# Tokens split at 256 of 544 instead of 272, with the work list ordered anew

## The chip, the cores and the metric

The kernel runs on one core of a Trainium2 chip. The metric is the device time of one execution in microseconds (us), the median of several runs. TensorE (PE) multiplies matrices, VectorE (DVE), ScalarE (ACT) and GpSimd (POOL) do element-wise work, SyncE (SP) issues the transfers.

## The reference

One decoder step of two layers over 512 prompt tokens and 8 x 4 sample tokens, 544 tokens in all, model width 1024. Cut to its core:

```
for each of 2 layers:
    mod = silu(c) @ w_mod + b_mod            # six vectors: sh1 sc1 g1 sh2 sc2 g2
    h   = rmsnorm(x) * (1 + sc1) + sh1
    z   = h @ w_in                           # q, k, v | S5 inputs | convolution inputs
    mixed = [windowed attention | S5 state space | gated convolution + layer norm]
    x   = x + g1 * (mixed @ w_out)
    h2  = rmsnorm(x) * (1 + sc2) + sh2
    x   = x + g2 * ((silu(h2 @ w_gate) * (h2 @ w_up)) @ w_down)     # width 2816
y = rmsnorm(x)
```

## The kernel before, in words

Everything lies transposed: features on the 128 partitions, the 544 tokens along the columns. `x` is eight tiles of 128 x 544. The big products keep near-float32 accuracy by splitting both factors into a high and a low part (`fp32r`); `mm3` (L603) issues three matmuls for one product of a 128 x 128 weight block with a run of tokens: high x high, high x low, low x high. The tokens are processed in two parts, `HALVES` (L29), each of `TH` = 272 columns. `mtiles` (L608) makes one or two output tiles of one part: for every block of the contraction and every output tile, one `mm3`. The weights come in chunks of 128 x 1024 (`raw`), are rounded to `hi` by ACT or DVE, and `lo` is the difference, on POOL or DVE (`split`, L584).

The second part holds the 32 sample tokens besides prompt tokens; where these need other modulation vectors, instructions are split at `PB`, the number of prompt tokens in the second part (240 before).

A norm takes these steps for each part. `stat_tile` (L685) squares a tile of `x` and adds it to `acc`. `rstd_of` (L712) sums over the partitions and puts tokens on partitions: for every group of 128 tokens in `GRP` (L700) one matmul with the squares as the weights and a single column of ones. With 272 tokens there are three groups, at 0, 128 and 144, which overlap. Some twelve short DVE instructions (`inv_sqrt`) make the inverse root of three columns. Then one matmul per group spreads it back over all partitions, the third group with 16 columns only. `make_h` (L734) multiplies and modulates the eight tiles and splits them into high and low. There are five norms: at the start, before the feed-forward of each layer, before the second layer, and at the end.

Within a layer: `project` makes the 12 column tiles of z, and between them, in the order that `STEPS` (L219) gives, stand `s5`, `taps`, the two convolutions `c0` and `c1`, `attn`, and the convolution's layer norm `norm`. The output projection contracts `mix`: tiles 0 and 1 are S5, 2 to 5 attention, 6 and 7 the convolution, in this order. It and the down projection take the last three tiles of the first part and then the last three of the second part (`SEQ_END`, L1482), so that the first part's norm can run beside the second part's matmuls. The last pair of the feed-forward's start is arranged likewise: two column tiles of the first part, then two of the second.

The order of all instructions on each engine is made when the program is built. `_schedule` (L225) is a list scheduler with estimated costs (`_cost`, L154): an instruction's rank is its longest path to the end plus a lift that its stage was given (`LIFTS`, L216, in ns). When an engine is free, the ready instruction of highest rank goes next; where two engines may take it, the scheduler picks one. `MODS` (L210) says which pairs of the six modulation vectors are computed together. Where PE has nothing ready for 60 ns, the scheduler puts in filler matmuls on the tile `zeros` (L627), so a wait of PE that the scheduler foresees appears in the trace as filler, not as idle time. Almost every instruction has the line L111 in the profile, that of the recording helper, so the rows below are told apart by tile names and shapes. A float32 matmul that isn't fp32r stands in the trace as two instructions.

Of the kernel before, what the change touches and what calls it, by code (L numbers as in the profile page):

```python
# [13 lines left out]
I32 = mybir.dt.int32  # L14
# [5 lines left out]
P = 128  # L20
# [3 lines left out]
NP = 512  # L24
# [1 line left out]
NT = 4  # L26
T = NP + NB * NT
TH = T // 2
HALVES = ((0, TH), (TH, T))  # L29
PB = NP - TH  # L30
DFF = 2816
MF = DFF // P
FH = MF // 2
# [185 lines left out]
STEPS = (((0, 1, 2), "taps", (3,), "c0", (4,), (5,), (6,), (7,), (8,), (9,), "s5", "attn", (10, 11), "c1", "norm"),  # L219
# [5 lines left out]
def _schedule(order, tags):  # L225
# [110 lines left out]
    wait = [len(d) for d in dep]  # L336
    bank = [sorted({a.tensor.name for a in o[1] + o[2] if a.space == PSUM}) for o in ops]
    lock = {}
    pick, why, last_dep, slot_by, freed_by, prev_end, prev_op = [0] * N, {}, {}, {}, {}, {}, {}
    engs = sorted({e for o in ops for e, _ in o[0]})  # L340
    pool = {e: [] for e in engs}
# [15 lines left out]
    while done < N - len(spare):  # L357
        progress = True
        while progress:
            progress = False  # L360
            for e in engs:
# [1 line left out]
                    continue  # L363
                best = None
                for r, i in pool[e]:
                    if not all(len(free[tags[n][0]]) > min(bisect.bisect_left(todo[tags[n][0]], nth[n]), RESERVE.get(tags[n][0], 99))
                               for n in touch[i] if n not in held):
                        continue
                    p = [o[0] for o in ops[i][0]].index(e)
                    key = -r  # L370
                    late = max((lock[b][0] for b in bank[i] if b in lock and lock[b][1] != e), default=0.0)
                    if late > now:
                        heapq.heappush(ev, (late, -1, 2))
                        continue
                    if len(ops[i][0]) > 1:
                        here = now + cost[i][p]
                        if port[i][p]:
                            here = max(here, held_port["Pool" if e == "DVE" else "DVE"] + cost[i][p])
                        if any(max(at[o[0]], now) + sum(cost[v][0] for w, v in pool[o[0]] if w < r) + cost[i][q] < here + (MARGIN if q < p else 0.0)
                               for q, o in enumerate(ops[i][0]) if q < p):  # L380
                            continue
                    if e == "ACT":
                        f = _TABLES.get(ops[i][3][p].get("func"))
                        if f and table not in f:
                            key -= 3000.0
                    if best is None or key > best[0]:
                        best = (key, r, i, p)
                if best is None and e == "PE" and FILL and spare and NWU <= issued < reals and now >= at[e] + (0.0 if filled else FILL):
                    late = max((lock[b][0] for b in bank[spare[-1]] if b in lock and lock[b][1] != e), default=0.0)
                    if late > now:  # L390
# [104 lines left out]
def tile_decoder_step(ctx: ExitStack, tc: tile.TileContext, I, O, order, dbg=None, stop=99):  # L495
# [26 lines left out]
    def small(cols, tag, bufs=2, dt=F32):  # L522
        return new(sm, [P, cols], dt, tag, bufs)

    def wt_(n=TH):
        return small(TH, "w", bufs=NWT)[:, :n]
# [80 lines left out]

    def mtiles(blks, acts, *hs):  # L608

        pss = [[mbank()[:, :TH] for _ in blks] for _ in hs]  # L610
        n = len(acts)
        order.stream = True
        for k in range(n):
# [71 lines left out]
    def stat_tile(acc, k, h):  # L685
# [1 line left out]
        if k == 0:  # L687
            act(acc, x[k][:, c0:c1], AF.Square)
        elif isinstance(acc, list):
            acc.append(wt_())  # L690
            act(acc[-1], x[k][:, c0:c1], AF.Square)
        else:
            sq = wt_()
            act(sq, x[k][:, c0:c1], AF.Square)
            tt(acc, acc, sq, ADD, eng=VG)

    def new_acc(h):
        return small(TH, f"acc{h}", bufs=1)

    GRP = (0, P, TH - P)  # L700

    def inv_sqrt(v, r, t, si, steps):

# [8 lines left out]
    def rstd_of(acc, n=D, last=False):  # L712


        bk = mbank()
        parts = acc if isinstance(acc, list) else [acc]
        for i, a_ in enumerate(parts):
            for g, o in enumerate(GRP):
                PE.matmul(out=bk[:, 4 * i + g:4 * i + g + 1], lhsT=a_[:, o:o + P], rhs=ones[:, 0:1], start=True, stop=True)
        v, r, t = (small(3, f"rs{i}") for i in range(3))  # L720
        ts(v, bk[:, 0:3], 1.0 / n, MUL, EPS, ADD)
        for i in range(1, len(parts)):
            stt(v, bk[:, 4 * i:4 * i + 3], 1.0 / n, v, MUL, ADD)
        if last:
            V.reciprocal(out=t, in_=v)
            act(r, t, AF.Sqrt)
        inv_sqrt(v, r, t, None if last else small(3, "rsi", dt=I32), 1 if last else 3)
        out = bk[:, P:P + TH]
        for g, o in enumerate(GRP):
            c = 0 if g < 2 else 2 * P - o  # L730
            PE.matmul(out=out[:, o + c:o + P], lhsT=r[:, g:g + 1].broadcast_to((P, P)), rhs=ident[:, c:], start=True, stop=True)
        return out

    def make_h(hp, rs, gt, modT, vsh, h):  # L734
        c0, c1 = HALVES[h]
        for k in range(KD):
            t = wt_()
            tt(t, x[k][:, c0:c1], rs, MUL, eng=V if rs.space == PSUM else VG)
            hf = wt_()
            npc = TH if h == 0 else PB  # L740
# [260 lines left out]
    rs0 = [rs0[:, i * TH:(i + 1) * TH] for i in range(2)]  # L1001
    for h in range(2):
        cp(rs0[h], rstd_of(accs[h]))
    prm, taps = ssm_params(0)
# [11 lines left out]
    for l in range(L):  # L1016
# [32 lines left out]

        def rope(out, ps, h):  # L1050
            c0, c1 = HALVES[h]
            sw = wt_()
            for b in range(4):
                cp(sw[32 * b:32 * b + 32], ps[32 * (b ^ 1):32 * (b ^ 1) + 32])
            t = wt_()
# [4 lines left out]
        def glu_out(i, h, pa, pg_):  # L1060

            c0 = HALVES[h][0]
            th = wt_()
            act(th, pg_, AF.Tanh, scale=0.5)
            ts(th, th, 0.5, MUL, 0.5, ADD, eng=VG)
            n, j0 = (TH if h == 0 else PB), CB + c0 // CS
# [7 lines left out]
        def z_out(role, h, ps):  # L1074
            c0, c1 = HALVES[h]
            i = int(role[1])
            if role[0] == "u":
                n = TH // 4 if h == 0 else PB // 4
# [387 lines left out]

        def resid(m, h, ps, gv):
            c0, c1 = HALVES[h]
            n = TH if h == 0 else PB
# [30 lines left out]
        for hf in range(2):  # L1500
# [2 lines left out]

            def gate_up(m, h, pss):
                c0, c1 = HALVES[h]
                sg = wt_()
                act(sg, pss[0], AF.Silu)
                av = wt_()
                tt(av, sg, pss[1], MUL)
                hi = at[m][0][:, c0:c1]  # L1510
                cp(hi, av)
# [27 lines left out]

    for h in range(2):  # L1540
        c0, c1 = HALVES[h]
        o = [page()[:, :4 * TH].rearrange("p (k t) -> p k t", k=4) for _ in range(2)]
        order.lift = FLIFT * (1 - h)
        for k in range(KD):
            act(o[k // 4][:, k % 4], x[k][:, c0:c1], AF.Copy, scale=par[0][:, A_GF + k:A_GF + k + 1])
        rs = rstd_of(accs[h], last=True)
        rsc = wt_()
        cp(rsc, rs)
        for k in range(0, KD, 2):
            v = o[k // 4][:, k % 4:k % 4 + 2]  # L1550
            if k == 4:
                tt(v, v, bc(rsc, 1, 2), MUL, eng=G)
            else:
                tt(v, v, bc(rs, 1, 2), MUL)
        for k in (0, 2, 6, 4):
            Q.dma_start(out=O["y"][:, k:k + 2, c0:c1], in_=o[k // 4][:, k % 4:k % 4 + 2])

    order.issue(tc)

# [190 lines left out]
```

## Time and profile before

| | us |
|---|---|
| median of 3 runs | 1311.04 |
| lowest, highest | 1310.49, 1311.4 |
| the profiled execution | 1313.35 |
| its span, first to last instruction | 1311.5 |
| PE busy in it | 1295.5 |
| DVE, ACT, POOL busy | 723.6, 431.5, 368.6 |

The profiled execution's time is its span and 1.85 us around it, and lies 2.3 us above the median. A busy PE counts fillers as work and each group of overlapping matmuls from the first start to the last end.

### The profile page before, as it was taken

The page shows a single profiled execution, that of the slowest core. Times are in us where ns is not written, and L with a number is a line of the kernel's source. Part 1 is how long each engine was busy: PE and PEld are TensorE (multiplying, and loading weights), DVE is VectorE, ACT ScalarE, POOL GpSimd, SP SyncE. Part 2 cuts the span into 40 slices and gives each one's busy share as a digit, 9 for nine tenths or more (in the row PEclk, how much of TensorE's full clock was granted, in tenths as well). Part 3 has the DMA queues.
Part 4 walks back from the last instruction along what each step waited for, and adds up shares of the span by engine and source line. Part 5 has one row for each costly group of instructions (what it writes and reads, how often), then busy time and mean ns, then how long its engine had stood idle before and what let it go on. Part 6 is the DMA issues. An engine that isn't in the chain of part 4 may idle for free.

```text
span 1311.5 us, 25293 instructions
## 1 busy us (share of the span) xinstructions
PE 1295.5 (99%) x10328; PEld 1219.6 (93%) x10328; DVE 723.6 (55%) x1674; ACT 431.5 (33%) x928; POOL 368.6 (28%) x455
## 2 busy tenths in 40 slices
PE   8999999999999999999999999999999999999997
PEld 7888768999999999999988897899999999999997
DVE  6868884676743357433447868657434323344343
ACT  4533471453221122212226346345312112122232
POOL 8653220248432033322012412022223202233101
PEclk9998999999999999999999999999999999999999
DMA  9886785523222223223366672231232222232322
GB/s 333 288 278 210 235 235 197 182 101 97 97 83 96 81 81 97 95 75 105 108 213 233 229 279 69 95 99 49 97 97 96 82 81 83 95 97 81 97 65 69
DMA packets 79654, 176.56 MB, mean 135 GB/s; under 512 B 22769, under 2 KB 40497, under 8 KB 79537
## 3 DMA queue, kind: packets, MB, share of 16 engines
q1 hardware_dynamic: 79536, 174.94, 40.6%
q8 instruction: 81, 1.33, 0.4%
q14 instruction: 37, 0.30, 0.1%
HBM read 164.22 MB, written 10.70 MB: 133 GB/s over the span
## 4 chain that ended last, share of the span: by engine, by line
PE 90%; DVE 3%; DMA 2%; POOL 2%; issue 1%; SPq 1%; ACT 1%; POOLq 0%; ACTq 0%; DVEq 0%
PE ps_s L111 86%; PE mod_s L111 4%; DVE pg_s L111 2%; POOL sp_s L111 1%; SPq L111 1%; POOL pg_s L111 1%; DVE sp_s L111 1%; DMA raw_s<-w_in 1%; DMA wm_s<-w_mod 1%; DMA pg_s<-d_s 0%; DMA conv_out<-pg_s 0%; ACT pg_s L111 0%; DMA pg_s<-ssm 0%; POOL w_s L111 0%; POOLq L1743 0%
## 5 line engine op out<-in xcount | busy, mean ns | idle before, releaser
L111 PE MATMUL ps_s<-pg_s,hi_s 128*128 128x272 f32 x5504 | 1050.8, 290 | 1.4 <-DVE pg_s L111 1.1
L111 PEld LDWEIGHTS ps_s<-pg_s,hi_s 128*128 128x128 f32 x5504 | 865.1, 189 | 18.6 <-issue 13.8
L111 PE MATMUL ps_s<-pg_s,lo_s 128*128 128x272 f32 x2752 | 791.2, 289 | 0.0
L111 PEld LDWEIGHTS ps_s<-pg_s,lo_s 128*128 128x128 f32 x2752 | 518.7, 189 | 7.0 <-issue 6.9
L111 POOL TENSOR_TENSOR lo_s<-raw_s,hi_s 128x1024 fp32r<-128x1024 f32 x77 | 223.3, 2903 | 657.8 <-DVE hi_s L111 372.0
L111 ACT ACTIVATE hi_s<-raw_s 128x1024 fp32r<-128x1024 f32 x128 | 135.0, 1059 | 356.2 <-PE ps_s L111 313.6
L111 DVE TENSOR_TENSOR lo_s<-raw_s,hi_s 128x1024 fp32r<-128x1024 f32 x95 | 119.7, 1261 | 63.9 <-ACT hi_s L111 62.4
L111 DVE TENSOR_TENSOR pg_s<-w_s,pg_s 128x272 fp32r<-128x272 f32 x148 | 113.3, 775 | 37.4 <-ACT pg_s L111 37.0
L111 PE MATMUL ps_s<-pg_s,pg_s 128*128 128x104 f32 (+10 forms) x864 | 123.5, 317 | 2.9 <-DVE nmx_s L111 1.7
L111 ACT ACTIVATE w_s<-ps_s 128x272 f32<-128x272 f32 (+1 forms) x178 | 69.0, 388 | 165.0 <-PE ps_s L111 145.6
L111 PEld LDWEIGHTS ps_s<-pg_s,pg_s 128*128 128x128 f32 (+4 forms) x864 | 97.1, 182 | 27.5 <-issue 12.5
L111 DVE CAST hi_s<-raw_s 128x1024 fp32r<-128x1024 f32 x44 | 30.4, 695 | 157.0 <-PE ps_s L111 157.0
L111 DVE SCALAR_TENSOR_TENSOR x<-ps_s,modT_s,x 128x272 f32<-128x272 f32 (+1 forms) x96 | 45.8, 482 | 105.9 <-PE ps_s L111 105.7
L111 ACT ACTIVATE pg_s<-w_s 128x272 fp32r<-128x272 f32 x149 | 61.7, 426 | 85.0 <-DVE w_s L111 82.6
L111 DVE TENSOR_TENSOR w_s<-w_s,ps_s 128x272 f32<-128x272 f32 x88 | 38.2, 434 | 69.9 <-ACT w_s L111 69.8
L111 ACT ACTIVATE pg_s<-ps_s 128x512 f32<-128x512 f32 (+11 forms) x100 | 35.2, 382 | 65.3 <-PE ps_s L111 63.5
L111 ACT ACTIVATE w_s<-x 128x272 f32<-128x272 f32 x70 | 29.0, 427 | 69.1 <-DVE x L111 61.3
L111 PE MATMUL mod_s<-wm_s,silu_c 128*32 128x512 f32 x320 | 46.9, 616 | 1.4 <-DMA wm_s<-w_mod 1.4
L111 DVE TENSOR_TENSOR acc_s<-acc_s,w_s 128x272 f32<-128x272 f32 x64 | 34.1, 548 | 18.4 <-ACT w_s L111 17.5
L111 POOL TENSOR_TENSOR acc_s<-acc_s,w_s 128x272 f32<-128x272 f32 x5 | 4.6, 912 | 138.8 <-ACT w_s L111 138.7
L111 ACT ACTIVATE w_s<-w_s,modT_s,gain_s 128x272 f32<-128x272 f32 (+1 forms) x64 | 35.9, 591 | 14.3 <-DVE w_s L111 11.3
L111 DVE TENSOR_TENSOR pg_s<-pg_s,pg_s 128x256 f32<-128x256 f32 (+4 forms) x78 | 37.8, 540 | 0.5 <-ACT pg_s L111 0.3
(139 smaller groups left out, 795.3 us busy)
## 6 DMA issues: line engine op xcount, KB each, us to landing
wm_s<-w_mod SPq DMA_DIRECT2D x80, 512.0 KB, 4.6
raw_s<-w_gate SPq DMA_DIRECT2D x44, 512.0 KB, 3.5
raw_s<-w_up SPq DMA_DIRECT2D x44, 512.0 KB, 3.9
raw_s<-w_down SPq DMA_DIRECT2D x44, 512.0 KB, 3.5
raw_s<-w_in SPq DMA_DIRECT2D x24, 512.0 KB, 6.1
pg_s<-cwt SPq DMA_DIRECT2D x20, 512.0 KB, 6.1
pg_s<-w_mod SPq DMA_DIRECT2D x32, 256.0 KB, 6.0
raw_s<-w_out SPq DMA_DIRECT2D x16, 512.0 KB, 4.0
```

The costliest lines, as they stand in the source:

```text
L111: r = real(*a, **k)
```

## The change

- `HALVES` becomes 0 to 256 and 256 to 544. `TA` = 256 replaces `TH` as the size of the first part, `TW` = 288 is the size of the second, and `PB` becomes 256. Small buffers (`w`, `acc`) are 288 columns wide. The S5 output stage keeps its own width of 272.
- In `rstd_of` the groups follow from the part's size: the first part has two (0 and 128), the second three (0, 128 and 160, the third spread with 32 columns).
- The final output of each part lies in four pages of two tiles instead of two pages of four.
- The scheduler's cost of an fp32r matmul becomes `n / 2.4 + 11.9` ns instead of `max(n / 2.4 + 2.5, 125.2)`; at 272 columns both are 125.2.
- `LIFTS` and `MODS` have new values, so the whole order is different.
- The test whether an instruction's tiles can be had is written as a function, with the same outcome, and a search loop ends early for engines other than ACT.

```
-TH = T // 2
-HALVES = ((0, TH), (TH, T))
-PB = NP - TH
+TA = 2 * P
+TW = T - TA
+HALVES = ((0, TA), (TA, T))
+PB = NP - TA
...
-            return max(n / 2.4 + 2.5, 125.2)
+            return n / 2.4 + 11.9
...
-MODS = ((4, 3), (2, 5)), ((4, 3), (2, 5)), ((0, 1),)
+MODS = ((2, 3), (4, 5)), ((2, 3), (4, 5)), ((0, 1),)
...
-LIFTS = dict(s5=44e3, attn=283e3, c1=60e3, c0=20e3), dict(s5=116e3, attn=64e3, norm=93e3, c1=170e3)
+LIFTS = dict(s5=222e3, attn=48e3, c1=60e3, c0=231e3, norm=218e3), dict(s5=116e3, attn=37e3, norm=93e3, c1=203e3, out=235e3)
...
-    GRP = (0, P, TH - P)
...
+        nt = _cols(parts[0])
+        grp = [min(o, nt - P) for o in range(0, nt, P)]
+        m = len(grp)
         for i, a_ in enumerate(parts):
-            for g, o in enumerate(GRP):
+            for g, o in enumerate(grp):
                 PE.matmul(out=bk[:, 4 * i + g:4 * i + g + 1], lhsT=a_[:, o:o + P], rhs=ones[:, 0:1], start=True, stop=True)
...
-        out = bk[:, P:P + TH]
-        for g, o in enumerate(GRP):
-            c = 0 if g < 2 else 2 * P - o
+        out = bk[:, P:P + nt]
+        for g, o in enumerate(grp):
+            c = g * P - o
             PE.matmul(out=out[:, o + c:o + P], lhsT=r[:, g:g + 1].broadcast_to((P, P)), rhs=ident[:, c:], start=True, stop=True)
...
-        o = [page()[:, :4 * TH].rearrange("p (k t) -> p k t", k=4) for _ in range(2)]
+        o = [page()[:, :2 * (c1 - c0)].rearrange("p (k t) -> p k t", k=2) for _ in range(4)]
```

## Rows read from the trace of the kernel before

**Rows 1.** The page: busy us, share of span, instructions of each engine.
```profile
PE 1295.5 (99%) x10328; PEld 1219.6 (93%) x10328; DVE 723.6 (55%) x1674; ACT 431.5 (33%) x928; POOL 368.6 (28%) x455
```

**Rows 2.** Groups by shape, PE, whole span: count | busy us, mean ns | idle before.
```profile
L111 PE MATMUL ps_s<-pg_s,hi_s 128*128 128x272 f32 x5504 | 1050.8, 290 | 1.4 <-DVE pg_s L111 1.1 <-ACT pg_s L111 0.3
L111 PE MATMUL ps_s<-pg_s,lo_s 128*128 128x272 f32 x2752 | 791.2, 289 | 0.0
...
L111 PE MATMUL ps_s<-cst,acc_s 128*128 128x1 f32 x60 | 7.8, 230 | 0.0
L111 PE MATMUL ps_s<-cst,rs_s 128*128 128x128 f32 x40 | 6.7, 282 | 0.0
...
L111 PE MATMUL ps_s<-cst,rs_s 128*128 128x16 f32 x20 | 2.9, 222 | 0.0
```

**Rows 3.** Busy time by stretch, feed-forward: stretch, length, busy (instructions) of each engine.
```profile
core 0: us, PE busy (x) PEld busy (x) DVE busy (x) ACT busy (x) POOL busy (x), PEclk, DMA share, GB/s
1100.00:1230.00 130.00, 130.00 (x1036) 130.00 (x1035) 49.92 (x66) 27.94 (x53) 35.75 (x11) 1.00 0.28 90
480.00:640.00 160.00, 160.00 (x1279) 160.00 (x1278) 76.38 (x139) 35.54 (x66) 46.87 (x34) 1.00 0.28 91
```

**Rows 4.** PE in order of time, second layer: start us, length us, what, count.
```profile
726.51 3.94 PE L111 MATMUL ps_s<-pg_s,pg_s 128*128 128x136 f32 x32
...
826.98 9.97 PE L111 MATMUL ps_s<-pg_s,pg_s 128*128 128x104 f32 x88
836.78 0.36 PE L111 MATMUL ps_s<-cr_s,cst 128*128 128x72 f32 x2
```

**Rows 5.** Fillers (tile zeros) by stretch; the PE column is their busy time.
```profile
20.00:60.00 40.00, 9.02 (x58) 7.58 (x58) 0.00 (x0) 1.00 0.93 308
98.00:118.00 20.00, 2.36 (x14) 2.17 (x14) 0.00 (x0) 0.83 0.71 237
230.00:242.00 12.00, 3.33 (x26) 3.07 (x26) 0.00 (x0) 1.00 0.71 216
272.00:280.00 8.00, 3.82 (x26) 3.23 (x26) 0.00 (x0) 1.00 0.85 295
690.00:697.00 7.00, 1.29 (x8) 1.06 (x8) 0.00 (x0) 0.76 0.69 264
893.00:900.00 7.00, 5.55 (x44) 5.16 (x44) 0.00 (x0) 1.00 0.58 180
```

**Rows 6.** DVE and POOL in order of time, norm before the first feed-forward.
```profile
268.32 2.28 DVE L111 SCALAR_TENSOR_TENSOR rs_s<-rs_s,rs_s 128x3 f32<-128x3 f32 x1
...
268.19 2.40 POOL L111 TENSOR_TENSOR lo_s<-raw_s,hi_s 128x1024 fp32r<-128x1024 f32 x1 [9.85 <-ACT hi_s L111]
```

**Rows 7.** PE in order of time at both feed-forward norms.
```profile
266.46 0.28 PE L111 MATMUL ps_s<-cst,acc_s 128*128 128x1 f32 x2
...
275.04 0.74 PE L111 MATMUL ps_s<-cst,rs_s 128*128 128x128 f32 x6
...
893.60 3.06 PE L111 MATMUL mod_s<-cst,zeros 128*128 128x128 f32 x26
896.50 0.74 PE L111 MATMUL ps_s<-cst,rs_s 128*128 128x128 f32 x6
```

**Rows 8.** In order of time, end of the first layer's mixer, several engines.
```profile
200.44 0.93 DVE L111 TENSOR_TENSOR pg_s<-ps_s,pg_s 64x64 fp32r<-64x64 f32 x4 [1.46 <-ACT pg_s L111]
...
208.20 0.66 DVE L111 SCALAR_TENSOR_TENSOR pg_s<-wu_s,pg_s 128x272 fp32r<-128x272 f32 x1 [0.76 <-ACT pg_s L111]
...
236.06 1.63 ACT L111 ACTIVATE pg_s<-pg_s,par 128x576 f32<-128x576 f32 x2
...
234.96 2.94 PE L111 MATMUL mod_s<-cst,zeros 128*128 128x128 f32 x24
237.66 1.02 PE L111 MATMUL ps_s<-pg_s,hi_s 128*128 128x272 f32 x6
```

**Rows 9.** Busy time by stretch where the granted clock (PEclk) is below 1.
```profile
98.00:113.50 15.50, 15.40 (x108) 12.52 (x106) 14.34 (x38) 8.95 (x22) 6.65 (x9) 0.78 0.72 239
...
689.50:695.80 6.30, 6.30 (x43) 6.30 (x43) 6.10 (x21) 6.21 (x15) 3.82 (x9) 0.74 0.85 313
```

**Rows 10.** DVE and POOL in order of time, after the last matmul of the stream.
```profile
1304.52 1.99 DVE L111 TENSOR_TENSOR pg_s<-pg_s,ps_s 128x544 f32<-128x544 f32 x3 [1.27 <-PE ps_s L111]
...
1307.09 1.33 POOL L111 TENSOR_TENSOR pg_s<-pg_s,w_s 128x544 f32<-128x544 f32 x1 [7.43 <-ACT w_s L111]
```

More of the change, by code (lines that the diff above doesn't have):

```diff
@@ L338, in _schedule, with placeable @@
     lock = {}
+    needs = [[(n, tags[n][0], nth[n]) for n in t] for t in touch]
+    def placeable(i):
+        for n, t, m in needs[i]:
+            if n not in held:
+                f = len(free[t])
+                if not f or f <= RESERVE.get(t, 99) and f <= bisect.bisect_left(todo[t], m):
+                    return False
+        return True
     pick, why, last_dep, slot_by, freed_by, prev_end, prev_op = [0] * N, {}, {}, {}, {}, {}, {}
@@ L365, in _schedule @@
                 for r, i in pool[e]:
-                    if not all(len(free[tags[n][0]]) > min(bisect.bisect_left(todo[tags[n][0]], nth[n]), RESERVE.get(tags[n][0], 99))
-                               for n in touch[i] if n not in held):
+                    if not placeable(i):
                         continue
@@ L387, in _schedule @@
                         best = (key, r, i, p)
+                    if e != "ACT":
+                        break
                 if best is None and e == "PE" and FILL and spare and NWU <= issued < reals and now >= at[e] + (0.0 if filled else FILL):
@@ L523, in small, with wt_ @@
         return new(sm, [P, cols], dt, tag, bufs)
-    def wt_(n=TH):
-        return small(TH, "w", bufs=NWT)[:, :n]
+    def wt_(h):
+        return small(TW, "w", bufs=NWT)[:, :HALVES[h][1] - HALVES[h][0]]
     def stt(out, in0, scalar, in1, op0, op1, eng=None):
@@ L608, in mtiles @@
     def mtiles(blks, acts, *hs):
-        pss = [[mbank()[:, :TH] for _ in blks] for _ in hs]
+        pss = [[mbank()[:, :HALVES[h][1] - HALVES[h][0]] for _ in blks] for h in hs]
         n = len(acts)
@@ L689, in stat_tile @@
         elif isinstance(acc, list):
-            acc.append(wt_())
+            acc.append(wt_(h))
             act(acc[-1], x[k][:, c0:c1], AF.Square)
         else:
-            sq = wt_()
+            sq = wt_(h)
             act(sq, x[k][:, c0:c1], AF.Square)
@@ L697, in new_acc @@
     def new_acc(h):
-        return small(TH, f"acc{h}", bufs=1)
-    GRP = (0, P, TH - P)
+        return small(TW, f"acc{h}", bufs=1)[:, :HALVES[h][1] - HALVES[h][0]]
     def inv_sqrt(v, r, t, si, steps):
@@ L716, in rstd_of @@
         parts = acc if isinstance(acc, list) else [acc]
+        nt = _cols(parts[0])
+        grp = [min(o, nt - P) for o in range(0, nt, P)]
+        m = len(grp)
         for i, a_ in enumerate(parts):
-            for g, o in enumerate(GRP):
+            for g, o in enumerate(grp):
                 PE.matmul(out=bk[:, 4 * i + g:4 * i + g + 1], lhsT=a_[:, o:o + P], rhs=ones[:, 0:1], start=True, stop=True)
-        v, r, t = (small(3, f"rs{i}") for i in range(3))
-        ts(v, bk[:, 0:3], 1.0 / n, MUL, EPS, ADD)
+        v, r, t = (small(3, f"rs{i}")[:, :m] for i in range(3))
+        ts(v, bk[:, 0:m], 1.0 / n, MUL, EPS, ADD)
         for i in range(1, len(parts)):
-            stt(v, bk[:, 4 * i:4 * i + 3], 1.0 / n, v, MUL, ADD)
+            stt(v, bk[:, 4 * i:4 * i + m], 1.0 / n, v, MUL, ADD)
         if last:
@@ L726, in rstd_of @@
             act(r, t, AF.Sqrt)
-        inv_sqrt(v, r, t, None if last else small(3, "rsi", dt=I32), 1 if last else 3)
-        out = bk[:, P:P + TH]
-        for g, o in enumerate(GRP):
-            c = 0 if g < 2 else 2 * P - o
+        inv_sqrt(v, r, t, None if last else small(3, "rsi", dt=I32)[:, :m], 1 if last else 3)
+        out = bk[:, P:P + nt]
+        for g, o in enumerate(grp):
+            c = g * P - o
             PE.matmul(out=out[:, o + c:o + P], lhsT=r[:, g:g + 1].broadcast_to((P, P)), rhs=ident[:, c:], start=True, stop=True)
@@ L736, in make_h @@
         for k in range(KD):
-            t = wt_()
+            t = wt_(h)
             tt(t, x[k][:, c0:c1], rs, MUL, eng=V if rs.space == PSUM else VG)
-            hf = wt_()
-            npc = TH if h == 0 else PB
+            hf = wt_(h)
+            npc = TA if h == 0 else PB
             act(hf[:, :npc], t[:, :npc], AF.Identity, bias=modT[:, vsh * 8 + k, 0:1], scale=gt[:, k, 0:1])
@@ L1000, in tile_decoder_step @@
     rs0 = page()
-    rs0 = [rs0[:, i * TH:(i + 1) * TH] for i in range(2)]
+    rs0 = [rs0[:, c0:c1] for c0, c1 in HALVES]
     for h in range(2):
@@ L1051, in rope @@
             c0, c1 = HALVES[h]
-            sw = wt_()
+            sw = wt_(h)
             for b in range(4):
                 cp(sw[32 * b:32 * b + 32], ps[32 * (b ^ 1):32 * (b ^ 1) + 32])
-            t = wt_()
+            t = wt_(h)
             tt(t, ps, cosT[:, c0:c1], MUL)
@@ L1062, in glu_out @@
             c0 = HALVES[h][0]
-            th = wt_()
+            th = wt_(h)
             act(th, pg_, AF.Tanh, scale=0.5)
             ts(th, th, 0.5, MUL, 0.5, ADD, eng=VG)
-            n, j0 = (TH if h == 0 else PB), CB + c0 // CS
+            n, j0 = (TA if h == 0 else PB), CB + c0 // CS
             def by_phase(a):
@@ L1077, in z_out @@
             if role[0] == "u":
-                n = TH // 4 if h == 0 else PB // 4
+                n = TA // 4 if h == 0 else PB // 4
                 pv = ps.rearrange("p (j s) -> p s j", s=4)
@@ L1468, in resid @@
             c0, c1 = HALVES[h]
-            n = TH if h == 0 else PB
+            n = TA if h == 0 else PB
             if h == 0:
@@ L1505, in gate_up @@
                 c0, c1 = HALVES[h]
-                sg = wt_()
+                sg = wt_(h)
                 act(sg, pss[0], AF.Silu)
-                av = wt_()
+                av = wt_(h)
                 tt(av, sg, pss[1], MUL)
@@ L1541, in tile_decoder_step @@
         c0, c1 = HALVES[h]
-        o = [page()[:, :4 * TH].rearrange("p (k t) -> p k t", k=4) for _ in range(2)]
+        o = [page()[:, :2 * (c1 - c0)].rearrange("p (k t) -> p k t", k=2) for _ in range(4)]
         order.lift = FLIFT * (1 - h)
         for k in range(KD):
-            act(o[k // 4][:, k % 4], x[k][:, c0:c1], AF.Copy, scale=par[0][:, A_GF + k:A_GF + k + 1])
+            act(o[k // 2][:, k % 2], x[k][:, c0:c1], AF.Copy, scale=par[0][:, A_GF + k:A_GF + k + 1])
         rs = rstd_of(accs[h], last=True)
-        rsc = wt_()
+        rsc = wt_(h)
         cp(rsc, rs)
         for k in range(0, KD, 2):
-            v = o[k // 4][:, k % 4:k % 4 + 2]
+            v = o[k // 2]
             if k == 4:
@@ L1555, in tile_decoder_step @@
         for k in (0, 2, 6, 4):
-            Q.dma_start(out=O["y"][:, k:k + 2, c0:c1], in_=o[k // 4][:, k % 4:k % 4 + 2])
+            Q.dma_start(out=O["y"][:, k:k + 2, c0:c1], in_=o[k // 2])
     order.issue(tc)
```

## The prediction

> **What bounds the kernel now.** I read the page's busy times first: PE is busy 99% of the span [rows 1]. That number hides waits, because the scheduler fills them with dummy matmuls. So I read next which shapes fill PE. The 8256 fp32r matmuls (5504 with high weights, 2752 with low ones) are the bulk [rows 2]. Their pitch follows from calm stretches of the feed-forward: a matmul lasts 0.29 us, so the number that touch a stretch is (length + 0.29) / pitch. 160.29 us over 1279 is 125.3 ns, 130.29 us over 1036 is 125.8 ns [rows 3]. 8256 times 125.4 ns is 1035 us, 79% of the span, and nothing but the matmuls themselves limits it. The rest is other PE work and waits. The third view is the fillers by stretch: after the start-up they stand at six places, 20 to 60, 98 to 118, 230 to 242, 272 to 280, 690 to 697 and 893 to 900 us, 25 us in sum [rows 5], where the third is the end of the first layer's mixer and the last three are norms. A tighter order can win some of these, plus what the clock costs (below). It can't win more.
>
> **The stream.** The change leaves the count of matmuls: 4128 now have 256 columns and 4128 have 288. If the pitch is a straight line in the columns over this range, the sum is what it was: the mean of the two sizes is 272. The trace has no fp32r matmul of another size, so I look at the nearest rows. Float32 matmuls of 136 columns stream at half the rate, so they occupy the array as long as 272 fp32r columns; their pitch is (3.94 - 0.28) / 31 = 118 ns. Those of 104 columns would stream in 87 ns, but 88 of them take 836.78 - 826.98 = 9.80 us, 111 ns each: that is the floor that a 128-column weight load sets [rows 4]. 125.4 is above both. So at 272 columns the matmul isn't held by that floor, and its cost is streaming at 2.4 GHz (113.3 ns) plus some 12 ns. On this line 256 columns take 118.7 and 288 take 132.1 ns, both over 111; the pair still sums to 250.8. I take 0. The bounds are wide. If fp32r has a floor of its own right at 125.4, the narrow matmul gains nothing and the wide one loses 6.7 ns: 4128 x 6.7 = +27.5 us. If the narrow one alone fell to the 111 ns floor: 4128 x (118.7 - 111) = -32 us. Neither end has a row for it, and both are kept as rivals with small chances.
>
> **The norms' own matmuls.** The first part drops from three groups to two. That is one column sum and one spread less per norm, each two instructions: 5 x 4 = 20 of the 120 that stand in [rows 2]. They have 128-column weights, so 111 ns each [rows 4]: 2.2 us. The first norm lies in the start-up, where PE waits anyway, so 4 x 0.45 = 1.8 us comes off PE's path (bounds 0 and 2.2). The DVE steps shrink from three columns to two, which is nothing for instructions of some 0.16 us fixed length.
>
> **Cover at the norms.** The first part's norm runs beside the second part's last three tiles. These are 72 matmuls in the output projection and 99 in the down projection; at 6.7 ns more each the cover grows by 0.5 us before each feed-forward and 0.7 us before layer 2. The fillers there say that PE waits for just this chain: its column sums start at 266.46 and its spread comes at 275.04 [rows 7], with 3.8, 1.3 and 5.6 us of fillers at the three norms [rows 5]. So about 0.5 + 0.5 + 0.5 = 1.5 us of them go (bounds: 0, and all of it). In turn the second part's norm has 96 narrow matmuls of cover instead of 96 of 272 columns, 0.6 us less each time. No filler stands there now, so I price this at nothing; if the slack is gone, it costs up to 1.9 us for the three norms.
>
> One thing in the chain is luck of the order: a DVE instruction of three columns took 2.28 us, while POOL made a low part for 2.40 us that began 0.13 us earlier [rows 6]. That is 2.1 us of a chain of 8. The Trainium skill (SBUF — State Buffer, section "SBUF: two separate sides") says that DVE and GpSimd hold a shared port pair as an exclusive lock for a whole instruction and the loser blocks; these rows agree with it, 2.28 against 0.16 us. The new order may meet such a collision or miss it at each norm: 2.1 us either way, taken as 0.
>
> **The new order of the first layer's mixer.** Before, attention finished first (200.44 + 0.93 us), then S5 (208.9), and the convolution's norm last: its silu starts at 236.06, and PE has run out of out-projection work that doesn't need it, with fillers from 234.96 to 237.66 [rows 8]. The convolution is thus 28 us behind the others. The change takes attention's lift from 283 to 48 us and raises S5, c0 and the norm, so the last column tiles and c1 overtake attention. Moving the convolution forward by 4 of those 28 us removes the wait. At stake is the 3.3 us of fillers [rows 5]; since the order is not known, I take two thirds, -2.2 us (bounds: -3.3, and the rival below). The queues it moves past: SP, which carries the convolution's round trip through DRAM, and ACT and DVE, where attention's softmax now waits behind S5. MODS only re-pairs the vectors; all four pairs' transfers and matmuls stay, and both pairs are needed before the first feed-forward: 0.
>
> **The tail.** After the last matmul the second part's work grows by 16 of 272 columns. The three multiplications (1.99 us) and POOL's (1.33 us) [rows 10] grow by 6%, 0.2 us, and the smaller steps some 0.1: +0.3 us. The four output pages instead of two hold the same columns: 0.
>
> **The clock.** It falls to 1.2 GHz twice inside the kernel: 15.5 us at a mean of 0.78 and 6.3 us at 0.74 [rows 9], that is (0.22 x 15.5) + (0.26 x 6.3) = 5.0 us of work lost. PE was busy in both with small matmuls. The new order moves them; it may avoid both (-5) or meet another such stretch (+3.4). I take 0.
>
> **The sum.** 0 - 1.8 - 1.5 - 2.2 + 0.3 = -5.2 us. Against the profiled execution, 1313.35 - 5.2 = 1308.2; that execution lies 2.3 us over the median, so the median goes from 1311.04 to 1305.8. I predict 1306.
>
> **The rivals.** A difference under 0.2% (2.6 us) is no change to a measurement of this kernel.
> First, the order only moves waits about: the mixer's 2.2 and the cover's 1.5 turn up at other places, and the norms' matmuls and the tail are left: 1311.0 - 1.8 + 0.3 = 1309.5. For it: the same number of dependent chains has to end before each feed-forward, and DVE is only 55% busy, so waits are latency.
> Second, slower: attention becomes the last chain of layer 1's mixer. The out projection contracts S5, attention, convolution in this order. While the convolution was last, six of eight blocks could run ahead, from 200 to 234 us; with attention last only two can. Five open tiles then give 5 x 2 x 3 = 30 matmuls or 3.8 us of cover instead of 5 x 6 x 3 = 90 or 11.3 us. The wait grows by up to 7.5 us: 1309.5 + 7.5 = 1317. It decides as soon as attention's last tile comes after the last column tile's matmuls are done by more than 3.8 us. Against it: in the second layer attention has a low lift already (64 us), and no fillers stand at the end of that mixer.
> Third, the floor of the stream at or near 272 columns: at its full price 1305.8 + 27.5 = 1333, at half of it 1320. [...]
> Fourth, its mirror image, a narrow matmul at the weight-load floor: below 1290.
>
> **How the numbers follow.** Forecast 0.49; waits moved about 0.24; attention last, with lost clock or port collisions of the same size, 0.19; a floor 0.05; the mirror image 0.03. Faster by over 0.2% is the forecast and the mirror image, 0.52; within it 0.24; slower 0.24. The range reaches down by what else the order can win, the rest of the norm fillers and one clock stretch: 1306 - 9 = 1297. Up it takes in attention at 1317 and one port collision: 1319. Outside lie the floor, the mirror image and the ends of the other cases.
>
> **What would show it.** The grouped rows should have 50 column sums with `acc` instead of 60, and fp32r pitches near 119 and 132 ns; 125 for the 256-column ones is the floor. No fillers between 230 and 242 us would confirm the mixer; fillers beside attention's last softmax, with the clock down, would be the second rival. Fillers before the feed-forwards should fall by half a us each. Wrong beyond repair would be a stream whose total isn't 1035 us.

## The result, and the profile after

The changed kernel takes 1322.4 us where the kernel before, measured beside it, took 1311.2: ratio 1.0070 (95% interval 1.0052 to 1.0088; the two medians alone, of four executions each, would give 1.0085). Measured once more it was 1.0077 (1.0059 to 1.0095). So the change costs 9 to 11 us; I had predicted 1306 us and a gain of 5.

The stream first. Groups by shape on PE, changed kernel, whole span (count | busy us, mean ns | idle before; the helper's line is 113 here), to be read against [rows 2]:

```profile
L113 PE MATMUL ps_s<-pg_s,hi_s 128*128 128x288 f32 x2752 | 559.1, 296 | 0.3 <-DVE pg_s L113 0.3
L113 PE MATMUL ps_s<-pg_s,hi_s 128*128 128x256 f32 x2752 | 502.8, 283 | 1.4 <-ACT pg_s L113 0.7 <-DVE pg_s L113 0.4 <-ACT hi_s L113 0.2
...
L113 PE MATMUL ps_s<-cst,rs_s 128*128 128x128 f32 x40 | 7.0, 297 | 0.1
L113 PE MATMUL ps_s<-cst,acc_s 128*128 128x1 f32 x50 | 6.5, 229 | 0.0
L113 PE MATMUL ps_s<-cst,rs_s 128*128 128x32 f32 x10 | 1.7, 253 | 0.0
```

The column sums are 50 instead of 60 and the spreads 50 instead of 60, as the change says. For the pitch, PE in order of time in a calm stretch of the second layer's feed-forward (start us, length us, what, count), at the three starts of a run of 48 matmuls of one size:

```profile
1157.62 0.40 PE L113 MATMUL ps_s<-pg_s,hi_s 128*128 128x256 f32 x2
...
1163.29 0.43 PE L113 MATMUL ps_s<-pg_s,hi_s 128*128 128x288 f32 x2
...
1169.68 0.40 PE L113 MATMUL ps_s<-pg_s,hi_s 128*128 128x256 f32 x2
```

48 matmuls of 256 columns take 5.67 us, 118.1 ns each; 48 of 288 take 6.39 us, 133.1 ns each. The mean, 125.6, is the pitch of 272 columns before [rows 3]. The Trainium skill (TensorE: Matmul & The Clock Gate, section "Back-to-back issue gap") gives N / 2.4 + 2.5 ns, here 109.2 and 122.5 ns, for a matmul by itself, and says that in a stream where each matmul has its weight load this counts too little at small widths and too much at large ones. These rows lie 9 and 11 ns above it, and the rows decide.

Fillers by stretch in the changed kernel (the PE column is their busy time), against [rows 5]:

```profile
20.00:60.00 40.00, 13.67 (x102) 12.38 (x102) 0.00 (x0) 1.00 0.92 303
98.00:118.00 20.00, 0.00 (x0) 0.00 (x0) 0.00 (x0) 1.00 0.73 251
220.00:242.00 22.00, 2.39 (x20) 2.33 (x20) 0.00 (x0) 1.00 0.65 198
272.00:283.00 11.00, 3.02 (x22) 2.69 (x22) 0.00 (x0) 1.00 0.76 255
690.00:700.00 10.00, 0.00 (x0) 0.00 (x0) 0.00 (x0) 0.83 0.63 226
756.00:768.00 12.00, 2.39 (x20) 2.31 (x20) 0.00 (x0) 1.00 0.53 179
900.00:915.00 15.00, 5.84 (x48) 5.62 (x48) 0.00 (x0) 1.00 0.34 107
```

They fell a little at the end of the first layer's mixer, grew by 4.65 us in the start-up and came up at a new place, 756 to 768 us, in the second layer's mixer. Another 2.64 us stand at 140 to 220 us, in the first layer's mixer, where the kernel before has 0.38. In the second layer's mixer open waits come on top, 5.0 us between 695 and 815 us in place of 0.8 (lines below). The table has, from each trace, when the first matmul of a part's stream starts. The executions are single ones, and two of one kernel differ by up to 5.5 us at one place (taps_behind_s5 reaches the second layer's feed-forward at 905.7 us and, run again, at 911.2), so smaller differences are not to be read.

| kernel | first layer's feed-forward | second layer's input projection | second layer's feed-forward | last stream matmul | span |
|---|---|---|---|---|---|
| before | 277.9 | 689.6 | 899.8 | 1299.4 | 1311.5 |
| changed | 280.1 | 691.6 | 909.4 | 1309.1 | 1321.5 |
| old_order_256 | 277.1 | 689.7 | 899.4 | 1297.8 | 1310.2 |
| new_order_272 | 282.8 | 694.7 | 907.3 | 1305.8 | 1318.0 |
| l0_new_l1_old | 282.0 | 692.9 | 904.3 | 1302.7 | 1315.3 |
| l0_old_l1_new | 278.8 | 690.6 | 905.1 | 1304.0 | 1316.8 |
| taps_behind_s5 | 280.3 | 692.2 | 905.7 | 1305.4 | 1317.9 |
| l0_old_l1_new_taps | 277.0 | 688.9 | 901.8 | 1300.6 | 1313.4 |

Changed against before: 2.2 us late into the first feed-forward, 2.0 into the second layer, 9.6 into its feed-forward, 9.7 at the end; only the last two stand clear of that. The feed-forwards take what they took. In these two traces 7.6 of the 9.7 us lie between 690 and 909 us; the runs below divide the loss more evenly between the layers.

The largest single wait there, as the chain that ended last runs through it (start us, us, what):

```profile
777.88 8.41 DMA d_s<-pg_s
786.29 0.02 issue
786.30 0.02 SPq L113
786.32 0.03 issue
786.35 7.61 DMA pg_s<-d_s
793.96 0.14 issue
794.09 6.01 PE ps_s L113 x19
```

S5's result goes through DRAM and back, and PE's matmuls on it start when it has landed:

```profile
794.09 6.02 PE L113 MATMUL ps_s<-pg_s,pg_s 128*128 128x272 f32 x20 [2.77 <-DMA pg_s<-d_s]
```

In the kernel before PE has no DMA wait in that stretch at all; from 695 to 815 us it waits for one thing (us in total, times, longest):

```profile
PE ps_s L111 <- DVE nmx_s L111: 0.8, 1, 0.8
```

Why the write starts at 777.88 is on SP's queue (issue start, issue length), with the last ScalarE instruction that makes S5's result:

```profile
770.35 0.46 ACT L113 ACTIVATE pg_s<-ps_s 128x256 f32<-128x256 f32 x2 [0.82 <-PE ps_s L113]
```
```profile
765.72 0.33 SPq L113 DMA_DIRECT2D raw_s<-w_out  x1
766.11 2.01 SPq L113 DMA_DIRECT2D pg_s<-cwt  x2
...
769.92 5.91 SPq L113 DMA_DIRECT2D pg_s<-cwt  x1
775.88 0.57 SPq L113 DMA_DIRECT2D pg_s<-ck  x1
776.49 1.28 SPq L113 DMA_DIRECT2D pg_s<-cwt  x1
777.88 0.38 SPq L113 DMA_DIRECT2D d_s<-pg_s  x1
```

The result is there at 770.8. SP is by then inside the issue of a load of convolution taps that takes 5.91 us, where the weight load of the same 512 KB at 765.72 took 0.33, and two more DMAs stand before S5's. The write goes out 7.1 us late. The copy itself, 544 KB, takes no longer than before: 8.5 us from the write's issue to the read's and 7.6 us from there to the landing, where the kernel before has 8.0 and 8.9. The same five loads stand ahead of S5's write in the kernel before too, but they are spread out, from 754.83 us on, and the write goes out 2.5 us after its result (765.4):

```profile
764.16 2.11 SPq L111 DMA_DIRECT2D pg_s<-cwt  x2
...
767.90 0.39 SPq L111 DMA_DIRECT2D d_s<-pg_s  x1
```

In the changed kernel SP stands 7.3 us, up to 765.72, at the weight load ahead of the taps, which waits for POOL's low part (761.58 to 765.70 us); everything behind it is bunched.

### The profile page after: what moved, and what is told of

Its sections match the earlier page's. It is cut to its first block, busy times and chain, and to the rows that moved or that the text cites. A ratio compares the mean times of both kernels' runs of the same rounds, so it can differ in the third digit from the quotient of the medians.

```text
span 1321.5 us, 25377 instructions
## 1 busy us (share of the span) xinstructions
PE 1299.5 (98%) x10356; PEld 1221.9 (92%) x10356; DVE 716.0 (54%) x1662; ACT 432.7 (33%) x934; POOL 361.9 (27%) x459
## 4 chain that ended last, share of the span: by engine, by line
PE 85%; DMA 4%; DVE 3%; POOL 3%; issue 2%; ACT 2%; SPq 1%; POOLq 0%; ACTq 0%
PE ps_s L113 81%; PE mod_s L113 4%; POOL sp_s L113 2%; DVE pg_s L113 2%; DMA wm_s<-w_mod 1%; SPq L113 1%; DMA d_s<-pg_s 1%; DMA pg_s<-d_s 1%; ACT pg_s L113 1%; POOL lo_s L113 1%; ACT hi_s L113 0%; DMA conv_out<-pg_s 0%; POOL pg_s L113 0%; ACT w_s L113 0%; DMA pg_s<-ssm 0%
## 5 line engine op out<-in xcount | busy, mean ns | idle before, releaser
L113 PE MATMUL ps_s<-pg_s,hi_s 128*128 128x256 f32 (+1 forms) x5504 | 1051.8, 290 | 1.7 <-DVE pg_s L113 0.7
L113 PE MATMUL ps_s<-pg_s,lo_s 128*128 128x288 f32 (+1 forms) x2752 | 791.2, 289 | 0.9 <-POOL lo_s L113 0.9
L113 DVE TENSOR_TENSOR pg_s<-w_s,pg_s 128x256 fp32r<-128x256 f32 (+1 forms) x148 | 111.3, 759 | 46.4 <-ACT pg_s L113 45.7
L113 ACT ACTIVATE w_s<-ps_s 128x256 f32<-128x256 f32 (+3 forms) x178 | 69.2, 389 | 153.2 <-PE ps_s L113 136.1
L113 DVE SCALAR_TENSOR_TENSOR x<-ps_s,modT_s,x 128x256 f32<-128x256 f32 x96 | 45.6, 481 | 91.9 <-PE ps_s L113 91.5
L113 ACT ACTIVATE pg_s<-w_s 128x256 fp32r<-128x256 f32 (+1 forms) x150 | 62.6, 427 | 80.6 <-DVE w_s L113 80.2
L113 DVE TENSOR_TENSOR w_s<-w_s,ps_s 128x256 f32<-128x256 f32 (+1 forms) x88 | 38.2, 434 | 59.1 <-ACT w_s L113 58.9
L113 ACT ACTIVATE pg_s<-ps_s 128x512 f32<-128x512 f32 (+10 forms) x104 | 36.1, 384 | 74.6 <-PE ps_s L113 69.4
L113 ACT ACTIVATE w_s<-w_s,modT_s,gain_s 128x256 f32<-128x256 f32 x64 | 36.4, 590 | 13.8 <-DVE w_s L113 9.9
L113 ACT ACTIVATE pg_s<-pg_s,nms_s 128x256 f32<-128x256 f32 (+2 forms) x68 | 31.4, 464 | 18.3 <-issue 13.1
```

The costliest lines, as they stand in the source:

```text
L113: r = real(*a, **k)
```

## The experiments

A word on the ratios: beside the experiments the kernel before took 1313 to 1314 us in place of the 1311 that the expected times start from. So ratios are compared, not times. The helper's line number shifts by a few in these kernels.

**The order and the division taken apart.** The plan (the sequence of every engine, the choice of engine, the buffers) is made for one division and then carried over, instruction by instruction, to the program with the other. `_use` sets the division and, where given, LIFTS and MODS (OLD_LIFTS and OLD_MODS stand here for the values of before); `_traced` records a program; `_carried` renumbers a plan, and drops or adds the first part's third group of norm matmuls.

```diff
-    return program(_Order(_schedule(trace, trace.tiles)))
+    _use(2 * P + 16, OLD_LIFTS, OLD_MODS)
+    of = _traced(program)
+    plan = _schedule(of, of.tiles)
+    _use(2 * P)
+    return program(_Order(_carried(plan, of, _traced(program))))
```

That is old_order_256; new_order_272 is its mirror image.

> The tokens divided at 256, but every engine's instructions issued in the order that the kernel before has (the plan is made for the division at 272 with the old constants and then carried over instruction by instruction; the first part's third group of norm matmuls, which the division at 256 does not have, is dropped). Only the division differs from before. Theory A, the new order costs the time: the division alone gives the small terms of the prediction (2.2 us of TensorE work less, and about what the tail takes back), so 1307 to 1311 us, and TensorE does not wait 2.8 us for S5's round trip near 790. Theory B, the unequal halves themselves cost it: 1318 to 1324 us, with the loss of 8 to 10 us again between the start of the second layer's input projection and its feed-forward.

Measured: ratio 1.0004 (0.9985 to 1.0023).

> The tokens divided at 272 as before, but issued in the order that the changed kernel has (the plan made for 256 with the new constants, carried over; the third group's matmuls come right behind the second's; one matmul of the attention that needs a column of the other half is put behind what it reads). Only the order differs from before. Theory A (the order): 1322 to 1327 us, the changed kernel's time plus the 2.2 us of TensorE work that comes back. Theory B (the halves): 1309 to 1314 us.

Measured: 1.0064 (1.0042 to 1.0086), and PE's wait for S5's copy comes with the order:

```profile
793.40 3.90 PE L115 MATMUL ps_s<-pg_s,pg_s 128*128 128x272 f32 x16 [1.88 <-DMA pg_s<-d_s]
```

The division alone changes nothing that can be measured; the order alone costs nearly the whole loss. Theory B, unequal halves, is out. To see whether the division is worth the 2.2 us that I had counted, it was measured again.

> Division at 256 in the order of the kernel before, once more in more rounds, to settle whether the division alone is worth anything. The prediction's small terms: 1 to 3 us less than before, ratio 0.998 to 0.999. Rival, they are taken back by the second part's longer tiles or fillers: ratio 0.9995 to 1.0005.

Measured: 1.0002 (0.9988 to 1.0017). The gain of 0.17% that 2.2 us would be (0.9983) lies just outside both intervals. The 1.8 us that I had taken, less the tail's 0.3 (0.9989), lies inside them at their edge, so a gain of that size is neither shown nor quite excluded.

**What makes an order bad.** old_numbers_256 is the changed kernel with the LIFTS and MODS of before, new_numbers_272 the division of before with the new ones; both are planned anew.

```diff
-LIFTS = dict(s5=222e3, attn=48e3, c1=60e3, c0=231e3, norm=218e3), dict(s5=116e3, attn=37e3, norm=93e3, c1=203e3, out=235e3)
-MODS = ((2, 3), (4, 5)), ((2, 3), (4, 5)), ((0, 1),)
+LIFTS = dict(s5=44e3, attn=283e3, c1=60e3, c0=20e3), dict(s5=116e3, attn=64e3, norm=93e3, c1=170e3)
+MODS = ((4, 3), (2, 5)), ((4, 3), (2, 5)), ((0, 1),)
```

> The changed kernel planned anew with the constants of before (the lifts of both layers' steps and the pairs of the modulation). Theory A in its narrow form, that the new constants make the bad order: 1305 to 1312 us. Theory A in its wide form, that any order planned anew for the division at 256 moves waits about by some us in the mixers, whatever the constants: 1312 to 1325 us. Theory B (the halves): 1318 to 1324 us.

Measured: 1.0145 (1.0120 to 1.0170).

> The division at 272 as before, planned anew with the new lifts and modulation pairs. Theory A in its narrow form (the new constants are bad for either division): 1318 to 1327 us. Theory A in its wide form (an order fits only the division it was looked for): anything from 1312 to 1325 us. Theory B (the halves): 1309 to 1314 us.

Measured: 1.0149 (1.0125 to 1.0174). Both are worse than either kernel, and worse than expected. So the constants are not good or bad in themselves: each set fits the division that it came with. The third run asks whether any disturbance of the plan costs something. Its edit to the planner of the kernel before:

```diff
-            return max(n / 2.4 + 2.5, 125.2)
+            return n / 2.4 + 11.9
```

> The kernel before with one figure of its planner moved by a hair: a 272-column matmul is taken at 125.23 ns in place of 125.20 (the changed kernel's formula at 272 columns), all else as before, division included; the order that comes out departs from 61 us of the plan on. Wide form of theory A (an order planned anew moves waits about by some us, whatever made it anew): a difference of over 2 us to either side, 1300 to 1308 or 1314 to 1330 us. Narrow form (only the changed constants and the division make a bad order): within 2 us, 1309 to 1313 us.

Measured: 0.9999 (0.9982 to 1.0016). This falls in the narrow form's range, but it hardly tests the question. Compared by names and shapes, the two traces have the same order on SP's queue throughout, and of the 10328 matmul instructions on PE one stands elsewhere, at 775 us; on the other engines a few neighbours change places, as they do between two executions of one kernel. So the order that ran is nearly that of before, and whether an order that really differs can be had without a loss stays open: all the others here that were planned anew lose, 9 to 20 us.

**The layers.** Two plans are joined at the first stream matmul of the first layer's last feed-forward half: up to there one plan's sequence, behind it the other's, with buffers renumbered.

```diff
-    return program(_Order(_schedule(trace, trace.tiles)))
...
+    a, b = (new, plan_new), (old, plan_old)
...
+    return program(_Order(_spliced(a[1], b[1], to, to.marks[1])))
```

That is l0_new_l1_old; in l0_old_l1_new `a` and `b` change places.

> Division at 256 throughout; the changed kernel's order up to the first layer's last feed-forward half, from there on the order of the kernel before (the two plans joined there, buffers renumbered behind the joint). Theory A1, the two layers' losses are separate and can be read from the lag of one trace behind the other: 2 to 3 us over before, 1313 to 1316 us, and from 690 to 912 us no loss. Rival, what the first layer's order leaves behind (buffers, queues, clock) makes the second layer lose: 1318 to 1323 us.

Measured: 1.0024 (1.0007 to 1.0041), 3.2 us.

> Division at 256 throughout; the order of the kernel before up to the first layer's last feed-forward half, from there on the changed kernel's. Theory A1: the second layer's mixer alone loses 7 to 9 us, 1318 to 1322 us, with the wait for S5's round trip near 790 again. Rival, the second layer loses only behind the first layer's new order: 1310 to 1314 us.

Measured: 1.0026 (1.0013 to 1.0039), 3.4 us, less than the 7 to 9 expected. PE waits for S5's copy again, 1.7 us. So both layers' orders lose by themselves. The sum, 0.50%, is below the whole's 0.70 and 0.77%; the intervals allow them to be equal, and whether the rest is an interplay I can't say.

**S5's copy behind the taps.** The five tap loads of the second layer that stand ahead of S5's read on SP are issued behind it:

```diff
+    late = [i for i in taps if 7600 < seq.index(i) < k]
...
+    seq = [i for i in seq[:k + 1] if i not in late] + late + seq[k + 1:]
```

> The changed kernel with one edit of its order: the five loads of the second layer's convolution taps that stand on SP's queue ahead of and among S5's write and read of its DRAM copy (766 to 779 us in the changed kernel's trace) are issued behind the read. Theory A2, S5's write stands behind tap loads that fill the queues, and TensorE's 2.8 us of waiting at 791 and the half-clock stretch behind it come from that: 2.5 to 5 us less than the changed kernel, 1317 to 1320 us, S5's read landing by 787, no wait of TensorE for it. Rival, something else is late at the same place (the attention's or the convolution's data): 1321 to 1324 us, with another wait of 2 to 3 us between 785 and 815.

Measured: 1.0057 (1.0037 to 1.0076). SP's queue in this kernel:

```profile
769.31 2.02 SPq L115 DMA_DIRECT2D pg_s<-ck  x1
771.50 2.25 SPq L115 DMA_DIRECT2D d_s<-pg_s  x1
...
779.26 0.40 SPq L115 DMA_DIRECT2D pg_s<-d_s  x1
779.71 2.89 SPq L115 DMA_DIRECT2D pg_s<-cwt  x5
```

S5's write goes out 6.4 us earlier, its read 7.1. What PE waited for between 695 and 815 us, in the changed kernel and then in this one (us in total, times, longest):

```profile
PE ps_s L113 <- DMA pg_s<-d_s: 2.8, 1, 2.8
PE mod_s L113 <- DMA wm_s<-w_mod: 1.2, 2, 1.0
PE ps_s L113 <- DVE nmx_s L113: 1.0, 3, 0.6
```
```profile
PE mod_s L115 <- DMA wm_s<-w_mod: 1.3, 2, 1.1
PE ps_s L115 <- DVE nmx_s L115: 1.0, 3, 0.6
```

The wait is gone, and no other took its place. As the ratio's interval overlaps the changed kernel's, both were measured once more together, and the edit was put on l0_old_l1_new too.

> The changed kernel unaltered, as the partner of the next run on the same chip: 1.0052 to 1.0088 of the kernel before, as it was measured, some 1322 to 1325 us here.

> The changed kernel with the five tap loads behind S5's read, once more beside the changed kernel itself. Theory A2 (S5's copy held up on SP's queue costs what its trace lost there): 2 to 4 us under the changed kernel of the same call, a ratio lower by 0.0015 to 0.003. Rival (what it wins there is given back by the next late thing): a ratio within 0.001 of the changed kernel's.

Measured: 1.0077 (1.0059 to 1.0095) without the edit and 1.0055 (1.0035 to 1.0075) with it.

> Division at 256, the order of before up to the first layer's last feed-forward half, the changed kernel's from there on, with the five tap loads behind S5's read. Theory A2: l0_old_l1_new had 1.0026, of which 2 to 3.7 us go, so 1.0000 to 1.0012; what is left is the wait for the modulation's loads near 718 and 762 us (2.3 and 2.5 us in the changed kernel's trace). Rival: 1.0020 to 1.0035, as without the edit.

Measured: 1.0007 (0.9997 to 1.0018), against 1.0026 without it. The three pairs give 1.7, 2.9 and 2.5 us, all one way. By their intervals only the last is clear of nothing by itself; weighted together they give 2.4 us, between 0.8 and 4 (an estimate that takes the intervals as independent). The wait itself was 2.8 and 2.0 us in two traces of the changed kernel and 1.7 us in l0_old_l1_new. So the tap loads ahead of S5's copy are worth some 2.4 us, most of what the second layer's order loses by itself. What is left there is 0.9 us, and by the interval anything from nothing to 2.4. In the changed kernel's trace there is still a wait for modulation weights, and as fillers set before another such group:

```profile
719.46 1.05 PE L113 MATMUL mod_s<-wm_s,silu_c 128*32 128x512 f32 x4 [1.03 <-DMA wm_s<-w_mod]
...
762.42 2.39 PE L113 MATMUL mod_s<-cst,zeros 128*128 128x128 f32 x20
764.74 1.06 PE L113 MATMUL mod_s<-wm_s,silu_c 128*32 128x512 f32 x8
```

Each group's two buffers are loaded only once the group before has read them. More buffers would test this; that wasn't tried, nor was MODS changed without LIFTS.

**A mended order.** The chain that the prediction named, the convolution's norm as the last of the first layer's mixer [rows 8], was shortened in the old order, for both divisions. ScalarE in the kernel before:

```profile
234.77 1.28 ACT L111 ACT_TABLE_LOAD   x1 [16.37 <-DMA pg_s<-d_s]
```

The table for silu is loaded after the data has come, though ScalarE idles for 16 us before it.

```diff
+            if PRE and l == 0:
...
+                act(dum, ones[:, 0:1], AF.Silu)
...
+    late = [i for i in seq[w:r] if i in dma and tag(ops[i][1][0]) == "wm"]
+    idle = [i for i in seq[used:used + 30] if ops[i][6] == "fill"]
+    seq = [i for i in seq[:r + 1] if i not in late] + late + [i for i in seq[r + 1:] if i not in idle]
```

> The division at 256 in the order of the kernel before, with one place of that order mended: at the end of the first layer's mixer (225 to 240 us) the two loads of a modulation block go behind the two reads of the convolution's DRAM copy on SP's queue, a one-column Silu is put behind the convolution's last Square so that ScalarE's table is loaded while it waits for the data, and the 12 filler matmuls that the plan has there are dropped. Theory: the reads land 5.0 us after their issue there, against 3.1 us in the second layer, where no load stands among them, and the table load takes 1.28 us behind them; TensorE fills and waits 3.3 us. So 2.0 to 3.3 us less than the same order unmended: 1307 to 1311 us where that gives 1311 to 1313. Rival, the modulation block that now comes later takes the bound over: 0 to 1 us less.

Measured: 0.9998 (0.9986 to 1.0011).

> The kernel before with the same three edits, division at 272. Theory: 2.0 to 3.3 us less than the kernel before, ratio 0.9975 to 0.9985, as much as at 256. If the division itself is worth what its 20 matmuls of the norms take (2.2 us), this stands 1 to 2 us over the same at 256; if not, level with it.

Measured: 1.0001 (0.9990 to 1.0013). The place itself did what was meant; SP, ScalarE and PE of better_272:

```profile
227.59 1.14 SPq L116 DMA_DIRECT2D pg_s<-d_s  x2
228.83 13.45 SPq L116 DMA_DIRECT2D wm_s<-w_mod  x6
...
230.68 0.87 ACT L116 ACTIVATE pg_s<-pg_s,par 128x576 f32<-128x576 f32 x1 [11.15 <-DMA pg_s<-d_s]
232.46 0.87 ACT L116 ACTIVATE pg_s<-pg_s,par 128x576 f32<-128x576 f32 x1 [0.92 <-DMA pg_s<-d_s]
...
233.83 1.05 PE L116 MATMUL mod_s<-wm_s,silu_c 128*32 128x512 f32 x4 [0.17 <-DMA wm_s<-w_mod]
235.10 1.05 PE L116 MATMUL mod_s<-wm_s,silu_c 128*32 128x512 f32 x4 [0.22 <-DMA wm_s<-w_mod]
236.08 1.15 PE L116 MATMUL ps_s<-pg_s,hi_s 128*128 128x272 f32 x7
```

Silu starts at 230.7 in place of 236.1 [rows 8], but the out-projection resumes only 1.6 us earlier, because PE now waits for the modulation's weights, and again at 240.85 (0.52 us). The rival, 0 to 1 us less, fits: the chain behind it was almost as late. Neither version beats the kernel before.

## Why the prediction was wrong

**The stream** (0): right. 118.1 and 133.1 ns against the 118.7 and 132.1 of the straight line; the floor and its mirror image are out.

**The norms' own matmuls** (-1.8): the count was right, 20, but no gain shows. The division alone came out level, 1.0004 and 1.0002, with this gain less the tail's 0.3 us at the edge of the intervals. If it isn't there, taking the 20 as being on PE's path was the error; no run of its own shows where the 2 us go.

**Cover at the norms** (-1.5): not as forecast. In old_order_256, which has the longer cover, the norms have 26, 8 and 44 fillers, as [rows 5] has, with 3.73, 1.30 and 5.48 us: nothing went. In the changed kernel they have 3.02, 0 and 5.84 us. That is 1.8 us less in sum, near the number that I gave, but it is luck: not half a us at each norm, and a matter of the new plan. What I missed is that a filler is an instruction of the order and not idle time. With the order held PE works off the same number however long the cover is, and a new plan sets the number by its own estimate.

**The port collision** (0): it belongs to the order and is no chance of the execution. In the kernel before a short DVE step is held up at three norms, for 2.28, 1.73 and 2.28 us (at 268.32, 688.10 and 888.53 us), and old_order_256 has all three too; in the changed kernel one is left, 2.25 us at 901.62, beside a low part of POOL's from 901.45 on that takes 2.40. So here the new order is the better one, and it loses all the same.

**The new order** (-2.2): the step that failed, in sign and in scope. The order alone, with the division of before, costs 0.64% (new_order_272), some 8 us. I read one wait of the first layer and asked what of it would go. The convolution's norm stayed the last chain there (in the changed kernel silu's table is loaded at 236.91, and PE fills 2.39 us and waits 0.36 us behind that), and other places before the feed-forward lost more: the first layer's order costs 3.2 us net. In the changed kernel's trace the fillers grew by 4.65 us in the start-up and by 2.26 us between 140 and 220 us; which of the places keeps the loss wasn't tested, and that part of the cause stays open. The second layer's mixer had no term in my sum at all, though LIFTS[1] and MODS change it as well. I wrote that each queue moved past counts, named SP for the first layer and priced nothing; in the second the price was some 2.4 us for five loads of 512 KB around one copy of 544 KB.

**The tail** (+0.3): right. DVE's three multiplications and POOL's, against [rows 10]:

```profile
1314.31 2.08 DVE L113 TENSOR_TENSOR pg_s<-pg_s,ps_s 128x576 f32<-128x576 f32 x3 [1.29 <-PE ps_s L113]
...
1317.00 1.40 POOL L113 TENSOR_TENSOR pg_s<-pg_s,w_s 128x576 f32<-128x576 f32 x1 [8.42 <-ACT w_s L113]
```

From the last stream matmul to the end of the span it is 12.4 us in place of 12.1.

**The clock** (0): no term of the order can be read from it. The stretch at 98 to 113 us [rows 9] runs at 1.00 now, but 98 to 118 us is at 1.00 in both traces of old_order_256 too, and at 0.83 in l0_old_l1_new, which has the same order up to there. The second layer's start is still low, 688 to 698 us at 0.83. A new stretch follows PE's wait for S5, 785 to 812 us at 0.94 (1.6 us); in the same kernel run again it is at 1.00, though PE waits 2.0 us there. The changed kernel, and then the same run again:

```profile
785.00:812.00 27.00, 23.07 (x135) 18.11 (x134) 14.59 (x53) 13.42 (x46) 1.83 (x1) 0.94 0.38 142
785.00:812.00 27.00, 23.86 (x157) 19.52 (x157) 16.88 (x56) 13.67 (x46) 3.95 (x2) 1.00 0.38 139
```

**The rivals.** "The order only moves waits about" had the right mechanism, but was priced as if what is moved could only come out level. It has a size of its own: orders of the same work that were run here span 0.9998 to 1.0149, some 20 us. "Attention last" did not happen: its last step of the first layer is at 216.72 us in the changed kernel, the convolution's silu at 238.21. So the range, up to 1319, was too narrow on that side by one more such term, the second layer's.

## What to carry to other kernels

Where a change also has a planner make a new order, price the order as a term with its own spread, in every stage that the plan covers, and hold the old order for one run to see what the change itself does: here it did nothing that could be measured, and the order cost 8 to 10 us. Where a plan is disturbed on purpose, compare the orders in the traces before reading the time: hair_272 had hardly a new one. On a queue that serves all transfers, look what stands ahead of each copy that a chain waits for; loads that aren't needed soon belong behind it. Filler instructions are part of the order, so a shorter chain behind them wins only what the next late chain allows.

## What the runs showed of the hardware

The granted clock between the layers differs from one execution of the same program to the next. Busy time by stretch from 685 to 705 us in old_order_256 and in the same kernel run again (the last columns are the granted clock, the DMA share and GB/s):

```profile
685.00:705.00 20.00, 20.00 (x168) 17.28 (x160) 18.44 (x71) 17.94 (x41) 5.75 (x9) 1.00 0.72 224
```
```profile
685.00:705.00 20.00, 20.00 (x132) 18.93 (x132) 14.04 (x52) 14.00 (x32) 5.75 (x9) 0.74 0.60 203
```

Full speed in one, and in the other 0.74, a mixture of 2.4 and 1.2 GHz; (1 - 0.74) x 20 = 5.2 us of work is an estimate of what that costs, and the two spans are 1310.2 and 1313.5 us. In both PE comes there from the last down projection, through the norm's small matmuls and fillers. So single traces are compared place by place here, and whole times only by ratios of many executions. The other surprise was a DMA issue on SP that itself took 5.91 us (4.24 in the same kernel run again), after three 512 KB loads and three smaller transfers had been issued within 4.2 us.
